# Two of four column blocks of an FFN down-projection by seven products in place of eight

## The chip, the cores and the metric

One Trainium2 chip, one of its cores. The metric is the device time of one execution in microseconds, as the median of several runs. TensorE (PE) multiplies matrices, VectorE (DVE), ScalarE (ACT) and GpSimd (POOL) work on elements, SyncE (SP) issues most DMAs. The profile adds PEld, TensorE's weight loads.

## The reference, cut to what matters

The program is a trunk of two layers on 256 positions and 2048 channels. Each layer has a mixer (pooling and attention in the first, an mLSTM in the second) and then the feed-forward network (FFN) that the change concerns; all of it is float32.

```
def conv_ffn(x, w_up, conv_w, conv_b, w_down):
    u = x @ w_up                                   # 2048 -> 2 x 5632
    up = jnp.pad(u, ((0, 0), (1, 1), (0, 0)))
    c = conv_w
    u = c[0] * up[:, :-2] + c[1] * up[:, 1:-1] + c[2] * up[:, 2:] + conv_b
    gate, val = jnp.split(u, 2, axis=-1)
    return (jax.nn.silu(gate) * val) @ w_down      # 5632 -> 2048
...
x = x + conv_ffn(rms_norm(x, norm_ffn[layer]), w_up[layer], conv_w[layer], conv_b[layer], w_down[layer])
```

## The kernel before

Every float32 operand of a product is split into a high part (a copy in TensorE's fp32r type) and a low part (the difference). A product is then three matmuls: high x high, high x low, low x high.

Weights come as a stream (class `Stream`, lines 65 to 108) of tiles of 128 partitions x 1024 columns, 512 KB each, in the order in which TensorE uses them. `load` issues a tile's DMA on SP into one of six buffers (tile `w`, line 80). `split` makes the high part on ScalarE (line 89) and the low part on VectorE (line 90) in one of four buffers (tile `hl`). So at most three split tiles stand ahead of the one that TensorE uses. `next` hands a tile to TensorE.

TensorE's order is that of the program, by hand; a small planner (`Weave`) puts the transposes and norm work of other tasks between the matmuls. The order on the other engines is written when the program is built, by a scheduler that places each instruction by a model of time; on the chip each engine then works through its list in order.

The FFN (`ffn_layer`, lines 877 to 962) has 44 feature blocks of 128, in chunks of 4, 8, 8, 8, 8, 8 (`FCH`). For each block, `up` (line 891) makes gate and value: `stat_group` (302) has four weight tiles, 64 matmuls of 512 or 256 columns, with the weights as the stationary operand; `gather` (363) joins the two partial sums from PSUM with a copy on ScalarE (366) and an addition on VectorE (367); line 895 multiplies by the norm R; line 899 applies the centre tap and the bias on ScalarE; lines 900 and 902 add the two outer taps on VectorE, once for the gate and once for the value; lines 905 to 908 make silu x value and split it into the chunk's tile `g`. `g` has two buffers, used by turns.

`down` (938) runs one chunk late: after the ups of chunk c come the four column blocks of 512 of chunk c-1 (the last chunk's follow at the end). For each column block and feature block, `mov_part` (325) has two row halves of 128 positions x three matmuls of 128x512 (tile `dn`), with activations stationary and weights moving; a weight tile holds two feature blocks, so it lasts 12 matmuls. `residual` (373) adds the sums into `x` on VectorE (376). PSUM has two pools of four banks: `mm`, two buffers of two banks, for up and down groups; `ps`, four buffers of one bank, for all smaller work. `_ffn_order` (1033) lists the weights in the same order.

Of the kernel before, what the change touches and what calls it, by code (L numbers as in the profile page):

```python
# [9 lines left out]
F32 = mybir.dt.float32  # L10
F32R = mybir.dt.float32r
AF = mybir.ActivationFunctionType
ALU = mybir.AluOpType
# [3 lines left out]
P = 128  # L17
D = 2048
S = 256
# [14 lines left out]
CH = 8  # L34
# [7 lines left out]
NB = D // 512  # L42
# [19 lines left out]
NC_ML = M_BG + 1  # L62


class Stream:


    def __init__(self, nc, wpool, spool, srcs, load_ahead, split_ahead):
        self.nc, self.wpool, self.spool, self.srcs = nc, wpool, spool, srcs
        self.la, self.sa = load_ahead, split_ahead  # L70
        self.w, self.hl = {}, {}
        self.n_load = self.n_split = self.at = 0

    def load(self, pieces=1):
        i = self.n_load
        width = self.srcs[i].shape[-1]
        n = width // pieces
        w = self.wpool.tile([P, CH * P], F32, tag="w", name=f"w{i}")
        for c in range(0, width, n):
            self.nc.sync.dma_start(w[:, c : c + n], self.srcs[i][:, c : c + n])  # L80
        self.w[i] = w, n, width
        self.n_load += 1

    def split(self, then=None):
        i = self.n_split
        w, n, width = self.w.pop(i)
        hl = self.spool.tile([P, 2, CH * P], F32R, tag="hl", name=f"hl{i}")
        for c in range(0, width, n):
            (self.nc.vector.tensor_copy if i + c == 0 else self.nc.scalar.copy)(hl[:, 0, c : c + n], w[:, c : c + n])  # L89
            self.nc.vector.tensor_sub(hl[:, 1, c : c + n], w[:, c : c + n], hl[:, 0, c : c + n].bitcast(F32))  # L90
            then and then(c // n)
        self.hl[i] = hl
        self.n_split += 1

    def ahead(self, i, split=None):
        n = len(self.srcs)
        while self.n_load < min(n, i + self.la + 1):
            if self.n_load >= self.n_split + self.la - self.sa + 1:
                self.split()
            self.load()  # L100
        while self.n_split < min(n, i + (self.sa if split is None else split) + 1):
            self.split()
# [54 lines left out]
def trunk(ctx: ExitStack, tc: tile.TileContext, gx, xT, xn, call, catt, cml, weights, out):  # L157
# [167 lines left out]
    def mov_part(ps, act, kts, first, last):  # L325

        n = len(kts)
        hl = None
        for i, k in enumerate(kts):
            if i % 2 == 0:  # L330
                hl = st.next()
            src, c = act(k), i % 2 * 512
            wh, wl = hl[:, 0, c : c + 512], hl[:, 1, c : c + 512]
            for t in range(2):
                xh, xl = (src[:, j, t * P : t * P + P] for j in range(2))
                mm(ps[:, t], xh, wh, first and i == 0, False)
                mm(ps[:, t], xh, wl, False, False)
                mm(ps[:, t], xl, wh, False, last and i == n - 1)
            wv.tick(1.29)
# [33 lines left out]
    def residual(ps, b, eng=None):  # L373
        for t in range(2):
            xs = x[:, t, b * 512 : b * 512 + 512]
            v.tensor_add(xs, xs, ps[:, t])
# [500 lines left out]
    def ffn_layer(layer, norm, nxt):  # L877
        with ExitStack() as es:
            def lp(name, bufs):
                return es.enter_context(tc.tile_pool(name=name, bufs=bufs, reuse_waits="tile"))  # L880

            tp = lp(f"ff{layer}", 2)

            def cw(tl, j):
                c = C_CONV + layer * 88 * 4 + tl * 4 + j
                return cst[:, c : c + 1]

            def xx(k):
                return norm.at(k)

            def up(f, gt, i):
                ps = stat_group(xx, list(range(KT)), f"up{layer}_{f}")
                wv.until(lambda: norm.R is not None)
                u = gather(tp, ps, f"up{layer}_{f}")
                v.tensor_mul(u, u, bc(norm.R, 2))  # L895
                y = tp.tile([P, 2, S], F32, tag="y", name=f"y{layer}_{f}")
                for j in range(2):
                    tl = f + j * FT
                    a.activation(y[:, j, :], u[:, j, :], AF.Identity, scale=cw(tl, 1), bias=cw(tl, 3))  # L899
                    v.scalar_tensor_tensor(y[:, j, 1:S], u[:, j, 0 : S - 1], cw(tl, 0), y[:, j, 1:S],  # L900
                                           ALU.mult, ALU.add)
                    v.scalar_tensor_tensor(y[:, j, 0 : S - 1], u[:, j, 1:S], cw(tl, 2), y[:, j, 0 : S - 1],  # L902
                                           ALU.mult, ALU.add)
                s_ = tp.tile([P, S], F32, tag="silu", name=f"s{layer}_{f}")
                a.activation(s_, y[:, 0, :], AF.Silu)
                v.tensor_mul(s_, s_, y[:, 1, :])
                a.copy(gt[:, i, 0, :], s_)
                v.tensor_sub(gt[:, i, 1, :], s_, gt[:, i, 0, :].bitcast(F32))

            def down_end(gt, b, kts):  # L910

                parts = [(0, 0, 512), (1, 0, 512)]
                pss = [psp.tile([P, 512], F32, tag="ps", name=f"end{i}") for i in range(2)]
                n = len(kts)

                def terms(i, k, hl):
                    t, c0, c1 = parts[i]
                    ps = pss[i][:, : c1 - c0]
                    wh, wl = (hl[:, j, k % 2 * 512 + c0 : k % 2 * 512 + c1] for j in range(2))
                    xh, xl = (gt[:, k, j, t * P : t * P + P] for j in range(2))  # L920
                    mm(ps, xh, wh, k == kts[0], False)
                    mm(ps, xh, wl, False, False)
                    mm(ps, xl, wh, False, k == kts[-1])

                for k in kts[:-2]:
                    if k % 2 == 0:
                        hl = st.next()
                    for i in range(2):
                        terms(i, k, hl)
                hl = st.next()  # L930
                for i, (t, c0, c1) in enumerate(parts):
                    for k in kts[-2:]:
                        terms(i, k, hl)
                    xs = x[:, t, b * 512 + c0 : b * 512 + c1]
                    v.tensor_add(xs, xs, pss[i][:, : c1 - c0])
                    nc.sync.dma_start(out[:, t, b * 512 + c0 : b * 512 + c1], xs)

            def down(c, gt, last):
                kts = list(range(FCH[c]))
                for b in range(NB):  # L940
                    if last and nxt is None and b == NB - 1:
                        down_end(gt, b, kts)
                        break
                    ps = mmp.tile([P, 2, 512], F32, tag="mm", name=f"dn{layer}_{c}_{b}")
                    mov_part(ps, lambda k: gt[:, k], kts, True, True)
                    residual(ps, b)
                    if last and nxt is None:
                        nc.sync.dma_start(out[:, :, b * 512 : b * 512 + 512], x[:, :, b * 512 : b * 512 + 512])
                    elif last:
                        nxt.add(b)  # L950

            wv.add(norm.finish(), 4.0)
            f, gts = 0, []
            for c, n in enumerate(FCH):
                gt = actp.tile([P, 8, 2, S], F32R, tag=f"B{c % 2}", name=f"g{layer}_{c}")
                gts.append(gt)
                for i in range(n):
                    up(f, gt, i)
                    f += 1
                if c:  # L960
                    down(c - 1, gts[c - 1], False)
            down(len(FCH) - 1, gts[-1], True)

    norms = [Norm(0), None]
    norms[1] = Norm(1)
# [16 lines left out]
def _mov(w):  # L982

    return w.reshape(-1, 2, P, 512).transpose(0, 2, 1, 3).reshape(-1, P, CH * P)
# [36 lines left out]
    return np.ascontiguousarray(t.transpose(4, 0, 2, 1, 3, 5)).reshape(FT * (KT // 4), P, CH * P)  # L1021


def _down_chunks(w):
    out, k0 = [], 0
    for n in FCH:
        rows = w[k0 * P : (k0 + n) * P]
        out += [_mov(rows[:, c : c + 512]) for c in range(0, D, 512)]
        k0 += n
    return np.concatenate(out)  # L1030


def _ffn_order():

    seq, u, d = [], 0, 0
    for c, n in enumerate(FCH):
        seq += [("u", u + i) for i in range(4 * n)]
        u += 4 * n
        if c:
            m = FCH[c - 1] // 4 * 8  # L1040
            seq += [("d", d + i) for i in range(m)]
            d += m
    m = FCH[-1] // 4 * 8
    seq += [("d", d + i) for i in range(m)]
    return seq


def _constants():
# [97 lines left out]
```

## Time and profile before

| | us |
|---|---|
| median of 3 runs (2206.41 to 2206.97) | 2206.9 |
| the profiled execution | 2206.69 |
| its span, first to last instruction | 2204.4 |
| TensorE busy in the span | 2199.3 |
| VectorE busy | 1525.3 |
| ScalarE busy | 1168.8 |
| matmuls of up groups (5632), busy | 984.2 |
| matmuls of down groups (2064), busy | 471.3 |
| low parts of weights on VectorE (772), busy | 939.0 |
| high parts of weights on ScalarE (771), busy | 806.1 |

The DMA queues moved 415.71 MB, 189 GB/s in the mean. A group line of the page reads: line of the kernel, engine, operation, tile written <- tiles read, partitions x elements, count | busy time in all, mean ns of one | idle time of the engine just before them, and who ended it. A line of the waits reads: who waited, for whom: us in all, times, the longest. A line of the view by windows gives the stretch, its length, and for each engine the busy time and the number of instructions, then the granted clock of TensorE, the busy share of the DMA engines and GB/s. The time that a matmul takes from issue to end (389 ns in the mean for a down matmul) is longer than the distance to the next one, since they are pipelined; the distance is what counts.

### The profile page before, as it was taken

The page shows a single profiled execution, that of the slowest core. Times are in us where ns is not written, and L with a number is a line of the kernel's source. Part 1 is how long each engine was busy: PE and PEld are TensorE (multiplying, and loading weights), DVE is VectorE, ACT ScalarE, POOL GpSimd, SP SyncE. Part 2 cuts the span into 40 slices and gives each one's busy share as a digit, 9 for nine tenths or more (in the row PEclk, how much of TensorE's full clock was granted, in tenths as well). Part 3 has the DMA queues.
Part 4 walks back from the last instruction along what each step waited for, and adds up shares of the span by engine and source line. Part 5 has one row for each costly group of instructions (what it writes and reads, how often), then busy time and mean ns, then how long its engine had stood idle before and what let it go on. Part 6 is the DMA issues. An engine that isn't in the chain of part 4 may idle for free.

```text
span 2204.4 us, 30654 instructions
## 1 busy us (share of the span) xinstructions
PE 2199.3 (100%) x11712; PEld 1888.3 (86%) x11712; DVE 1525.3 (69%) x2172; ACT 1168.8 (53%) x1666; POOL 28.1 (1%) x40
## 2 busy tenths in 40 slices
PE   9999999999999999999999999999999999999999
PEld 7888888888888888889888889888888888888887
DVE  7686677776776767666767677667777677676764
ACT  7665555554554545456555454555545455454542
POOL 0020000000000000000000000000000000000000
PEclk9999999999999999999999999999999999999999
DMA  9555566656566555656565655555666656566554
GB/s 324 177 165 168 176 191 188 191 188 197 184 194 187 191 192 191 197 171 207 162 197 178 186 180 168 185 180 188 188 191 190 196 186 192 190 191 191 192 191 143
DMA packets 118036, 415.71 MB, mean 189 GB/s; under 512 B 13082, under 2 KB 15426, under 8 KB 117890
## 3 DMA queue, kind: packets, MB, share of 16 engines
q1 hardware_dynamic: 114656, 409.76, 58.2%
q10 hardware_dynamic: 3074, 3.75, 0.8%
q8 instruction: 91, 1.49, 0.3%
q14 instruction: 55, 0.45, 0.1%
q0 software_dynamic: 160, 0.26, 0.0%
HBM read 411.58 MB, written 2.14 MB: 188 GB/s over the span
## 4 chain that ended last, share of the span: by engine, by line
PE 100%; DVE 0%; issue 0%
PE up L203 44%; PE dn L203 21%; PE op L203 8%; PE mv L203 4%; PE mq L203 4%; PE mk L203 4%; PE mo L203 4%; PE qproj L203 3%; PE kproj L203 1%; PE pool L203 1%; PE vproj L203 1%; PE qk L203 1%; PE av L203 1%; PE end L203 0%; PE xt L254 0%; PE sc L203 0%
## 5 line engine op out<-in xcount | busy, mean ns | idle before, releaser
L90 DVE TENSOR_TENSOR hl<-w,hl 128x1024 fp32r<-128x1024 f32 (+2 forms) x772 | 939.0, 1217 | 467.9 <-ACT hl L89 466.2
L89 ACT CAST hl<-w 128x1024 fp32r<-128x1024 f32 (+1 forms) x771 | 806.1, 1046 | 677.1 <-PE dn L203 242.6
L203 PE MATMUL up<-xx,hl 128*128 128x512 f32 (+1 forms) x5632 | 984.2, 337 | 0.0
L203 PEld LDWEIGHTS up<-xx,hl 128*128 128x128 f32 x5632 | 857.9, 188 | 125.8
L203 PE MATMUL dn<-hl,g 128*128 128x512 f32 x2064 | 471.3, 389 | 0.0
L203 PEld LDWEIGHTS dn<-hl,g 128*128 128x128 f32 x2064 | 386.3, 188 | 79.4
L366 ACT COPY tb_up<-up 128x512 f32<-128x512 f32 x88 | 51.7, 587 | 154.0 <-PE up L203 154.0
L367 DVE TENSOR_TENSOR tb_up<-up,tb_up 128x512 f32<-128x512 f32 x88 | 60.8, 691 | 97.1 <-ACT tb_up L366 97.1
L899 ACT ACTIVATE y<-tb_up,cst 128x256 f32<-128x256 f32 x176 | 96.4, 595 | 47.2 <-DVE tb_up L895 47.2
L203 PE MATMUL mk<-xx,hl 128*128 128x512 f32 (+1 forms) x512 | 92.2, 337 | 0.0
L203 PE MATMUL mq<-xx,hl 128*128 128x512 f32 (+1 forms) x512 | 92.1, 337 | 0.0
L203 PE MATMUL mv<-hl,xx 128*128 128x512 f32 (+2 forms) x480 | 91.7, 350 | 0.0
L203 PE MATMUL mo<-hl,xx 128*128 128x512 f32 (+1 forms) x480 | 91.6, 348 | 0.0
L203 PE MATMUL op<-hl,cat 128*128 128x512 f32 x384 | 91.6, 393 | 0.0
L203 PE MATMUL op<-hl,mcat 128*128 128x512 f32 x384 | 89.5, 392 | 0.0
L203 PEld LDWEIGHTS mq<-xx,hl 128*128 128x128 f32 x512 | 79.2, 188 | 11.6
L203 PEld LDWEIGHTS mk<-xx,hl 128*128 128x128 f32 x512 | 79.0, 188 | 11.4
L203 PEld LDWEIGHTS mv<-hl,xx 128*128 128x128 f32 x480 | 78.3, 189 | 11.2
L203 PEld LDWEIGHTS mo<-hl,xx 128*128 128x128 f32 x480 | 76.5, 190 | 10.6
L203 PEld LDWEIGHTS op<-hl,mcat 128*128 128x128 f32 x384 | 71.4, 188 | 14.6
L203 PEld LDWEIGHTS op<-hl,cat 128*128 128x128 f32 x384 | 70.9, 188 | 14.1
L902 DVE SCALAR_TENSOR_TENSOR y<-tb_up,cst,y 128x255 f32<-128x255 f32 x176 | 76.8, 477 | 0.0
(209 smaller groups left out, 1270.0 us busy)
## 6 DMA issues: line engine op xcount, KB each, us to landing
w<-in_up SPq DMA_DIRECT2D x352, 512.0 KB, 3.5
w<-in_dn SPq DMA_DIRECT2D x176, 512.0 KB, 3.7
w<-in_m_in SPq DMA_DIRECT2D x124, 512.0 KB, 4.0
w<-in_a_in SPq DMA_DIRECT2D x46, 512.0 KB, 4.5
w<-in_a_out SPq DMA_DIRECT2D x32, 512.0 KB, 3.5
w<-in_m_out SPq DMA_DIRECT2D x32, 512.0 KB, 3.4
w<-in_m_g SPq DMA_DIRECT2D x5, 432.0 KB, 3.4
x<-in_xn SPq DMA_DIRECT2D x4, 512.0 KB, 9.9
```

Of the source, the lines that this page charges most:

```text
L89: (self.nc.vector.tensor_copy if i + c == 0 else self.nc.scalar.copy)(hl[:, 0, c : c + n], w[:, c : c + n])
L90: self.nc.vector.tensor_sub(hl[:, 1, c : c + n], w[:, c : c + n], hl[:, 0, c : c + n].bitcast(F32))
L203: pe.matmul(out_, lhsT, rhs, start=start, stop=stop, skip_group_check=True)
L366: a.copy(tb, ps[:, :, 1, :])
L367: v.tensor_add(tb, ps[:, :, 0, :], tb)
L899: a.activation(y[:, j, :], u[:, j, :], AF.Identity, scale=cw(tl, 1), bias=cw(tl, 3))
L902: v.scalar_tensor_tensor(y[:, j, 0 : S - 1], u[:, j, 1:S], cw(tl, 2), y[:, j, 0 : S - 1], ALU.mult, ALU.add)
```

## The change

For all chunks but the last of each layer, the column blocks 2 and 3 (columns 1024 to 2047) are no longer done by `down`. A pair of feature blocks (k), the two row halves (t) and the two column blocks form a 2x2 by 2x2 product of blocks, which is done by a scheme of seven products with sums of blocks in place of eight products.

The combinations of activations (`combine`) are made on VectorE after every second up, and split by ScalarE and VectorE. The combinations of weights are made as the tiles come in: a tile `Sum` is one load on SP and a second load on POOL that adds to it in the DMA; a tile `Chain`, which follows it, gets two additions on VectorE before it is split. The seven products go into seven banks that gather over a whole chunk, in two passes: pass A (four products, one `Sum` and one `Chain` tile for each pair) and pass B (three products, one and a half plain tiles). A unit of pass A stands after each of the next chunk's first four ups, a unit of pass B after each of the other four. At a pass's end the banks are added into a tile `acc` (on VectorE; copied by ScalarE for the first chunk), and after the last chunk but one `total` adds the seven sums into `x`. The column blocks 0 and 1 keep the old scheme, and stand after the second and the fourth up of the next chunk (the first chunk has two pairs; its units and down groups follow half as many ups). The last chunk is done as before.

In `up`, the outer taps are now products on ScalarE (tile `z`, two more activations for the gate and two for the value) and two additions on VectorE that cover gate and value at once.

```
@@ class Stream
     def load(self, pieces=1):
+        src = self.srcs[i]
+        if isinstance(src, Sum):
+            i in self.w or self.prepare(i)
+            return
+        src = src.src if isinstance(src, Chain) else src
...
+    def prepare(self, i):
+        w = self.sums.tile([P, CH * P], F32, tag="sum", name=f"sum{i}")
+        self.nc.sync.dma_start(w, self.srcs[i].one)
+        self.nc.gpsimd.dma_start(w, self.srcs[i].other, accum_op=ALU.add)
+        self.w[i] = w, CH * P, CH * P
 
     def split(self, then=None):
         i = self.n_split
         w, n, width = self.w.pop(i)
+        if isinstance(self.srcs[i], Sum):
+            self.sum = w
+        elif isinstance(self.srcs[i], Chain):
+            half = CH * P // 2
+            self.nc.vector.tensor_add(w[:, :half], w[:, :half], self.sum[:, :half])
+            self.nc.vector.tensor_add(w[:, half:], w[:, half:], w[:, :half])
...
     def ahead(self, i, split=None):
         n = len(self.srcs)
+        for j in range(self.n_load, min(n, i + 10)):
+            if isinstance(self.srcs[j], Sum) and j not in self.w:
+                self.prepare(j)
@@ def ffn_layer
-            tp = lp(f"ff{layer}", 2)
+            tp, t1p, kp = lp(f"ff{layer}", 2), lp(f"ff1{layer}", 1), lp(f"ffk{layer}", 1)
+            st.sums = lp(f"ffs{layer}", 2)
...
+                z = t1p.tile([P, 2, 2, S], F32, tag="z", name=f"z{layer}_{f}")
                 for j in range(2):
                     tl = f + j * FT
+                    a.activation(z[:, 0, j, :], u[:, j, :], AF.Copy, scale=cw(tl, 0))
+                    a.activation(z[:, 1, j, :], u[:, j, :], AF.Copy, scale=cw(tl, 2))
                     a.activation(y[:, j, :], u[:, j, :], AF.Identity, scale=cw(tl, 1), bias=cw(tl, 3))
-                    v.scalar_tensor_tensor(y[:, j, 1:S], u[:, j, 0 : S - 1], cw(tl, 0), y[:, j, 1:S],
-                                           ALU.mult, ALU.add)
-                    v.scalar_tensor_tensor(y[:, j, 0 : S - 1], u[:, j, 1:S], cw(tl, 2), y[:, j, 0 : S - 1],
-                                           ALU.mult, ALU.add)
+                v.tensor_add(y[:, :, 1:S], y[:, :, 1:S], z[:, 0, :, 0 : S - 1])
+                v.tensor_add(y[:, :, 0 : S - 1], y[:, :, 0 : S - 1], z[:, 1, :, 1:S])
...
+            def combine(c, j, g4):
+                sf = t1p.tile([P, 4, P], F32, tag="sf", name=f"sf{layer}_{c}_{j}")
+                v.tensor_sub(sf[:, 0:2], g4[:, 0::3], g4[:, 1:2].to_broadcast([P, 2, P]))
+                v.tensor_add(sf[:, 2], sf[:, 1], g4[:, 0])
+                v.tensor_sub(sf[:, 3], sf[:, 2], g4[:, 2])
+                s3 = kp.tile([P, 2, 3, P], F32R, tag=f"s3{j}", name=f"s3{layer}_{c}_{j}")
+                s1 = st.sums.tile([P, 2, P], F32R, tag=f"s1{j}", name=f"s1{layer}_{c}_{j}")
+                for d, e in ((s3, sf[:, 0:3]), (s1, sf[:, 3])):
+                    a.copy(d[:, 0], e)
+                    v.tensor_sub(d[:, 1], e, d[:, 0].bitcast(F32))
...
+            def product(ps, xs, wh, wl, first, last):
+                xh, xl = xs
+                mm(ps, xh, wh, first, False)
+                mm(ps, xh, wl, False, False)
+                mm(ps, xl, wh, False, last)
+                wv.tick(0.68)
+
+            def unit(kind, c, j):
+                order = (4, 6, 5, 3) if kind == "A" else (0, 1, 2)
+                if j == 0:
+                    for e in order:
+                        pss[e] = psp.tile([P, 512], F32, tag="ps", name=f"pp{layer}_{c}_{e}")
...
+                for m, e in enumerate(order):
+                    if m % 2 == 0:
+                        hl = st.next()
+                    wh, wl = (hl[:, i, m % 2 * 512 : m % 2 * 512 + 512] for i in range(2))
+                    product(pss[e], xs[m], wh, wl, j == 0, j == n - 1)
+                if j == n - 1:
+                    for e in order:
+                        if c == 0:
+                            a.copy(acc[:, e], pss[e])
+                        else:
+                            v.tensor_add(acc[:, e], acc[:, e], pss[e])
+                    if kind == "B" and c == len(FCH) - 2:
+                        total()
+
+            def total():
+                p1, p2, p3, q4, p5, q6, p7 = (acc[:, e] for e in range(7))
+                x00, x01, x10, x11 = (x[:, t, c : c + 512] for t in range(2) for c in (1024, 1536))
+                v.tensor_sub(q6, q6, p1)
+                v.tensor_sub(p5, q6, p5)
+                for xs, op, e in ((x01, v.tensor_add, p5), (x01, v.tensor_sub, p3), (x11, v.tensor_add, p5),
+                                  (x11, v.tensor_sub, p7), (x10, v.tensor_sub, q6), (x10, v.tensor_add, p7),
+                                  (x10, v.tensor_add, q4), (x00, v.tensor_add, p1), (x00, v.tensor_add, p2)):
+                    op(xs, xs, e)
...
+def _ffn_plan():
+    seq = []
+    for c, n in enumerate(FCH):
+        pairs = FCH[c - 1] // 2 if c else 0
+        for i in range(n):
+            seq.append(("up", c, i))
+            if i < 2 * pairs:
+                seq.append(("AB"[i // pairs], c - 1, i % pairs))
+            for b in range(2):
+                if pairs and i == (b + 1) * pairs // 2 - 1:
+                    seq.append(("down", c - 1, b))
+    return seq + [("down", len(FCH) - 1, b) for b in range(NB)]
...
@@ weights of a pair, b11 to b22 its blocks of 128 x 512
+    return np.concatenate(out), two(b12, b12), two(b11, b22), two(b22, b21), two(b11, b21), b22
...
+        elif kind == "A":
+            out += [Sum(s0[q], s1[q]), Chain(r[q])]
+        else:
+            out += [ba[q], bb[q]]
```

## The prediction

> **What bounds the kernel now.** I read the page's chain first, then the waits of TensorE, then one stretch of the stage that the change touches, then the rows of the instructions concerned.
>
> ```profile
> PE 2199.3 (100%) x11712; PEld 1888.3 (86%) x11712; DVE 1525.3 (69%) x2172; ACT 1168.8 (53%) x1666; POOL 28.1 (1%) x40
> ...
> PE 100%; DVE 0%; issue 0%
> ```
>
> The chain of work that ended last is TensorE from end to end. The waits of TensorE alone confirm it: one wait, 1.2 us, in the whole execution.
>
> ```profile
> PE wps L227 <- DVE pad L595: 1.2, 1, 1.2
> ```
>
> So a matmul taken away shortens the run by its whole duration, as long as nothing else becomes late. The next view says how near the others are. Its middle row is one steady FFN chunk (eight up groups, four down groups); the other two are stretches in which VectorE is nearly or quite full.
>
> ```profile
> core 0: us, PE busy (x) PEld busy (x) DVE busy (x) ACT busy (x) POOL busy (x), PEclk, DMA share, GB/s
> 140.00:168.00 28.00, 28.00 (x176) 24.98 (x175) 25.54 (x50) 20.14 (x44) 9.00 (x11) 1.00 0.48 143
> 433.00:566.00 133.00, 133.00 (x708) 114.16 (x707) 91.20 (x120) 68.28 (x89) 0.00 (x0) 1.00 0.60 191
> 1092.00:1106.00 14.00, 14.00 (x65) 11.60 (x64) 14.00 (x13) 6.29 (x7) 0.00 (x0) 1.00 0.50 171
> ```
>
> The reader is to see that a chunk has VectorE 69% and ScalarE 51% busy at a granted clock of 1.00, and that TensorE stays full beside a VectorE at 91% (25.54 of 28 us, ScalarE 72%) and, for 14 us, at 100%. Four split tiles in flight carry it over such stretches. The prices come from the rows by shape, the page's down row, the chain's stretch of eight ups, the same chunk for the down tiles (`dn`) alone, and the DMA rows:
>
> ```profile
> L90 DVE TENSOR_TENSOR hl<-w,hl 128x1024 fp32r<-128x1024 f32 x762 | 930.6, 1222 | 464.5 <-ACT hl L89 462.8
> L902 DVE SCALAR_TENSOR_TENSOR y<-tb_up,cst,y 128x255 f32<-128x255 f32 x176 | 76.8, 477 | 0.0
> L895 DVE TENSOR_TENSOR tb_up<-tb_up,R 128x512 f32<-128x512 f32 x88 | 60.9, 692 | 3.0
> L908 DVE TENSOR_TENSOR g<-s,g 128x256 fp32r<-128x256 f32 x88 | 36.7, 417 | 0.0
> ```
> ```profile
> L203 PE MATMUL dn<-hl,g 128*128 128x512 f32 x2064 | 471.3, 389 | 0.0
> ```
> ```profile
> 413.14 89.16 PE up L203 x512
> ```
> ```profile
> 433.00:566.00 133.00, 43.69 (x192) 35.97 (x192) 5.14 (x8) 1.00 0.60 191
> ```
> ```profile
> L899 ACT ACTIVATE y<-tb_up,cst 128x256 f32<-128x256 f32 x176 | 96.4, 595 | 47.2 <-DVE tb_up L895 47.2
> ```
> ```profile
> w<-in_dn SPq DMA_DIRECT2D x176, 512.0 KB, 3.7
> ...
> R<-rr POOLq DMA_DIRECT2D x2, 128.0 KB, 6.5
> ```
>
> **The change, part by part.**
>
> *Removed on the path.* Per pair of feature blocks, two column blocks and two row halves cost 8 products of 3 matmuls; now 7. All chunks but the last hold 36 feature blocks, 18 pairs a layer, 36 in both: 36 x 3 = 108 matmuls of 128x512. The down row of the page gives 471.3 us / 2064 = 0.228 us each; in the chunk above the same tiles take 43.69 us for 192, also 0.228. 108 x 0.228 = **24.6 us**. The other products keep their shape and price.
>
> *VectorE.* From the rows, 1.07 ns per element on top of a fixed part: 0.28 us for 128 elements, 0.417 for 256, 0.555 for 384, 0.69 for 512, 1.222 for 1024. An up group: four low parts 4.89, gather and R 1.38, the two joined tap additions 2 x 0.69 (four of 0.477 before), gate and low part 0.83: 8.5 us. Each A unit adds two low parts and two chain additions, 2 x 1.222 + 2 x 0.69 = 3.8; each B unit 1.222 + 0.686 = 1.9; the combinations of a pair 0.417 + 3 x 0.28 + 0.555 = 1.8, half to each up; sums out of PSUM 7 x 0.685 = 4.8 a chunk; a down group 4 x 1.222 + 2 x 0.683 = 6.25. A chunk: 4 x (8.5 + 3.8 + 0.9) + 4 x (8.5 + 1.9 + 0.9) + 2 x 6.25 + 4.8 = 115.3 us. By the same means the old chunk is 97.2, where the view shows 91.20: successive instructions overlap a little, so times 0.938, **108 us**. TensorE's new chunk: 8 x 11.15 (89.16 us per eight ups in the chain) + 84 x 0.228 + 2 x 10.9 = 130.2 us. VectorE rises from 69% to 83%; an up with its A unit is the tightest, 13.2 x 0.938 = 12.4 of 13.9 us (89%), and the two down groups in the A pass give back 4.7 us each. That lies below the 91% over 28 us at which TensorE did not wait. The final sum (11 additions of 0.69, 7.6 us) falls beside the last chunk's four down groups, where VectorE has 4.7 us to spare in each.
>
> *ScalarE.* Four more activations per up (two per half, taken at 0.595, the row with two column operands; 0.47 would be the low end by the plain scaled rows), 1.5 more casts per pair, the two casts of the combinations at 0.8: a chunk goes from 71 to 100 us nominal, times 0.96 as before: 96 of 130 us, 74%. Hidden beside TensorE too. Behind the six activations of an up stand the casts of the next tiles, 6 x 0.595 = 3.6 us late at most; a tile's slot comes free three tiles ahead of its use, 8 us in ups, 5 where the short tiles of a unit lie between. If that cover were gone the price is 3.6 us per up at most.
>
> *SP and POOL.* 36 first loads of sums (512 KB) and 36 half tiles go on SP, 36 accumulating loads on POOL. In the order of instructions the first sums of each layer stand among the preceding output projection's loads, and wait there for the last head's operations; in the trace those end at 189.5 us, and the load behind it on SP left at 189.8, so nothing is held. Later sums wait for the buffer of the sum two before, which was split before the loads beside it in the queue may go. POOL's square roots stand behind the first two sums, over 60 us before they are due. Bytes: 36 x 1.25 MiB = 47 MB more; a chunk moves 25.3 + 5.2 = 30.5 MB in 130 us, 235 GB/s, and by the view's 0.60 at 190 a DMA share of 0.74 (0.77 in the A pass). The page's first slice moved 324 GB/s, so plain loads keep up.
>
> *The accumulating load* is in no row. From below: a plain load of the same bytes, 3.7 us. From above: POOL's 128 KB row taken in proportion, 4 x 6.5 = 26 us. I take 8, nearer to the first since 6.5 us for a quarter of the bytes must be mostly fixed. Its cover: of each chunk's four sums, two have a buffer early; the other two get theirs when the sum two before is split, and VectorE's chain addition stands behind the first split of the second-next up: about an up (less one tile), a unit, a down and one tile, 8.4 + 2.7 + 10.9 + 2.8 = 25 us, less 4 for the first load: 21 us, and 4 to 5 more until TensorE runs out of split tiles.
>
> *Sum.* 2206.7 us (the profiled execution; its span 2204.4, the median of the runs 2206.9) - 24.6 + 2.4 (one wait of the 1.2 us kind in each layer, where units begin) = **2184.5 us**.
>
> **The rivals.**
>
> *VectorE sets the pace of the stage.* In the old chunk it idled 41 us, nearly all of it for ScalarE:
>
> ```profile
> DVE hl L90 <- ACT hl L89: 30.8, 28, 1.6
> DVE tb_up L367 <- ACT tb_up L366: 8.8, 8, 1.1
> ```
>
> The new one has 130.2 - 108.2 = 22 us left. For: the joined tap additions wait for all six activations, and both engines run in a fixed order. Against: it idled because it was ahead, waiting for slots, and such waits shrink when it is late; the two full stretches above. If 24 us of waits stay, each of the nine chunk-equivalents (4.5 a layer) grows by 2 us, 18 in all: 2202 us; from 24.7 us on the gain is gone, and at 26 it is 2220.
>
> *The sums land late: slower.* Where the accumulating load takes more than 25.5 us from issue to landing, VectorE's in-order queue stands at the chain addition with the splits of the next tiles behind it, and TensorE follows. That is 2 sums in 4 chunks of 2 layers, 16 places; the gain is gone at 27 us, and at 28 it is 16 x 2.5 = 40 us: 2184.5 + 40 = about 2224. For: POOL's DMA rows are the slowest per byte, 6.5 us for 128 KB, and VectorE will be busier. Against: the 8 us estimate.
> The Trainium skill ("SBUF — State Buffer", section "Who interferes with whom") speaks for this rival: GpSimd writes such a DMA's descriptors, and VectorE operations that hold the shared port shut it out. Its strict form needs two-port operations, and these rows are all TENSOR_TENSOR; with two SBUF inputs it names a conflict with GpSimd reads only. The POOL rows agree in direction (6.5 against 3.7 us); no run here shows the cause.
>
> *It does not do what it says:* the short tiles of a unit could cost TensorE between products what eight products would. Nothing in the old rows shows it (op and dn, with the same three-matmul terms, both run at 0.23 us); 2200 to 2207.
>
> **How the numbers follow.** Forecast 0.57 (2182 to 2190); VectorE's pace 0.20 (half of it faster than 2202, a quarter on each side of 2211); late sums 0.20, nearly all slower; no effect 0.03. A measurement here tells 0.2% (4.4 us) from no change. Faster: 0.57 + 0.10 = 0.67; same: 0.05 + 0.01 + 0.03 = 0.09; slower: 0.05 + 0.19 = 0.24. The range runs from 2181 (no waits at all) to 2222; it leaves out half of the late sums, the worst of VectorE's pace, and little below.
>
> **What would show it.** Right: TensorE's waits still a few us, the products' tiles at 0.228 us per matmul, a VectorE of 80 to 85% in a chunk, chunks of 130 us. VectorE's pace: TensorE waiting for low parts (hl) all through the stage, chunks over 132 us. Late sums: VectorE idle at the chain additions, released by the accumulating DMA, landings over 25 us in the DMA rows. I am wrong if the chain of waits leaves TensorE for more than 10 us.

## The result, and the profile after

The changed kernel takes 2203.78 us (median of 20 runs, 2202.42 to 2206.86), the kernel before, beside it, 2206.58 us (20 runs, 2206.35 to 2206.97): a ratio of 0.9987, 95% interval 0.9981 to 0.9993. So 2.8 us are gained where 22.2 were forecast, and by the prediction's bound of 0.2% (4.4 us) that is no difference. The time lies in the range that was given, 2181 to 2222, but the forecast was wrong by 19.3 us.

The page of the changed kernel, in the same order as before: busy times, the clock by slices, and the shares of the chain of waits.

```profile
PE 2181.5 (99%) x11604; PEld 1871.5 (85%) x11604; DVE 1669.3 (76%) x2358; ACT 1374.3 (62%) x2176; POOL 59.2 (3%) x76
...
PEclk9999999999999999999999999999999999999998
...
PE 98%; DVE 1%; issue 0%; ACT 0%; DVEq 0%
```

108 matmuls are gone (x11712 to x11604), as the change says. The span fell from 2204.4 to 2201.9 us, but TensorE's busy time fell by 17.8. (It did not fall by the 24.6 of the 108 matmuls: what is left runs some 1.9 us slower, and some 24 matmuls ran at half the clock; both are shown below.) The clock's last slice is 8 where it was 9, and the chain, all TensorE before, now leaves it for some 2% of the span. TensorE's waits say where:

```profile
PE dn L237 <- ACT g L948: 15.2, 2, 7.6
PE wps L261 <- DVE pad L629: 1.2, 1, 1.2
```

Two waits of 7.6 us, one in each layer, for ScalarE's cast of the activations `g`; the 1.2 us one was there before. So there is one place to look at. The steady chunks are as forecast. The view by windows of one chunk (ups of eight blocks, units A and B, two down groups), and under it its two passes:

```profile
core 0: us, PE busy (x) PEld busy (x) DVE busy (x) ACT busy (x) POOL busy (x), PEclk, DMA share, GB/s
541.50:671.70 130.20, 130.20 (x694) 111.61 (x693) 106.96 (x144) 87.55 (x137) 3.44 (x4) 1.00 0.75 234
541.50:618.90 77.40, 77.40 (x401) 65.94 (x400) 66.36 (x88) 52.50 (x81) 3.44 (x4) 1.00 0.81 245
618.90:671.70 52.80, 52.80 (x294) 45.67 (x293) 40.60 (x57) 35.05 (x56) 0.00 (x0) 1.00 0.66 219
```

TensorE is full at a granted clock of 1.00, from the first `up` of the chunk to the first of the next in 130.2 us (forecast 130.2); VectorE is busy 107 us (forecast 108) and 86% in pass A. The load that no row had shown, and the load it adds to, in the DMA rows (last figure: median us from issue to landing):

```profile
sum<-in_dn SPq DMA_DIRECT2D x36, 512.0 KB, 4.7
sum<-in_dn POOLq DMA_DIRECT2D x36, 512.0 KB, 7.6
```

It lands after 7.6 us (taken at 8).

**The gap.** TensorE's timeline at the end of the first layer's ups (start, duration, operation, in brackets the wait ahead of it; `pp` are the products of a unit); the last up's matmuls end at 930.1 us:

```profile
929.95 1.53 PE L237 MATMUL pp<-hl,g 128*128 128x512 f32 x6
931.32 0.85 PE L237 MATMUL pp<-hl,s 128*128 128x512 f32 x3
932.00 9.68 PE L237 MATMUL dn<-hl,g 128*128 128x512 f32 x42
949.31 6.87 PE L237 MATMUL dn<-hl,g 128*128 128x512 f32 x18 [7.62 <-ACT g L948]
```

Behind the last up stand one unit B (9 matmuls) and then the last chunk's first down group. Its first seven feature blocks (42 matmuls) run; the eighth needs the last up's own activations. ScalarE has written their high part at 949.25 us, 19.1 us after the up's end, and VectorE the low part at 949.91, after 19.8. VectorE in these 19 us:

```profile
930.76 0.69 DVE L401 TENSOR_TENSOR tb_up<-up,tb_up 128x512 f32<-128x512 f32 x1 [1.10 <-ACT tb_up L400]
931.37 1.27 DVE L1000 TENSOR_TENSOR acc<-acc,pp 128x512 f32<-128x512 f32 x2
...
934.90 0.68 DVE L1008 TENSOR_TENSOR acc<-acc 128x512 f32<-128x512 f32 x1
935.50 0.68 DVE L1013 TENSOR_TENSOR x<-x,acc 128x512 f32<-128x512 f32 x1
936.11 2.35 DVE L121 TENSOR_TENSOR hl<-w,hl 128x1024 fp32r<-128x1024 f32 x2
...
939.58 0.68 DVE L941 TENSOR_TENSOR y<-y,z 128x510 f32<-128x510 f32 x1
...
943.05 1.89 DVE L1013 TENSOR_TENSOR x<-x,acc 128x512 f32<-128x512 f32 x3
944.86 0.68 DVE L942 TENSOR_TENSOR y<-y,z 128x510 f32<-128x510 f32 x1
945.46 1.22 DVE L121 TENSOR_TENSOR hl<-w,hl 128x1024 fp32r<-128x1024 f32 x1
946.60 1.89 DVE L1013 TENSOR_TENSOR x<-x,acc 128x512 f32<-128x512 f32 x3
948.40 0.41 DVE L947 TENSOR_TENSOR s<-s,y 128x256 f32<-128x256 f32 x1
```

The reader is to see two kinds of work in one list. The last up's own (L401, L933, L941, L942, L947, then L949) is short; between its pieces stand the eleven additions of the final sum (L1008, L1009, L1013), the three of the pass's banks (L1000) and six splits (L121). VectorE hardly pauses (it is busy 7.60 of 7.60 and 7.70 of 7.70 us in the windows further down). In the kernel before, the same place was (TensorE, then VectorE):

```profile
900.22 56.16 PE L203 MATMUL dn<-hl,g 128*128 128x512 f32 x247
```
```profile
908.10 0.42 DVE L908 TENSOR_TENSOR g<-s,g 128x256 fp32r<-128x256 f32 x1
```

The low part, last of the activations, was there 8.1 us after the up's end (900.4 us), and TensorE had four down groups of the chunk before (4 x 10.9 us) and seven blocks of the last chunk's first, some 53 us, to do meanwhile. The change took the path to the low part from 8.1 to 19.8 us, and its cover from 53 to 11.6.

**The clock behind it.** The view by windows around the gap:

```profile
934.00:941.60 7.60, 7.60 (x34) 6.01 (x33) 7.60 (x11) 5.24 (x8) 0.00 (x0) 1.00 0.56 180
941.60:949.30 7.70, 0.09 (x1) 0.00 (x0) 7.70 (x13) 0.82 (x2) 0.00 (x0) 0.68 0.66 226
949.40:954.50 5.10, 5.10 (x12) 3.99 (x13) 2.74 (x5) 2.20 (x4) 0.00 (x0) 0.50 0.19 60
954.70:957.00 2.30, 2.30 (x12) 1.88 (x11) 0.00 (x0) 0.79 (x1) 0.00 (x0) 1.00 0.53 116
```

The granted clock (the column before the DMA share) falls to 0.50 in the gap and stays there for 5.3 us behind it: 12 matmuls in 5.1 us, 0.427 each from start to start in place of 0.227, some 2.4 us more. In the trace the half clock lasts 10.24 us each time and begins 2.7 us into the gap. The Trainium skill ("TensorE: Matmul & The Clock Gate", Part 1) says that TensorE falls to half speed after an idle window of some 3.4 us and comes back after a busy one. The length agrees, with three times 3.41 us, and so does the return; the fall came earlier than an idle window of that length, 2.7 us into the gap, and in experiment 1 a wait of 1.8 us was enough.

A gap of 7.62 us between the end of one matmul and the start of the next puts their starts 8.0 us apart in place of 0.23, so it costs 7.8. Each gap costs 7.8 + 2.4 us, 20.4 in all, and 2203.8 - 20.4 = 2183.4 us would be the kernel without them. That is the theory: the final sum and the missing down groups together make the gap. The rivals: one of the two alone makes it, or the gap hides another cost that would come out once it is closed.

### The profile page after: what moved, and what is told of

It is laid out like the page before. It is cut to its first block, busy times and chain, and to the rows that moved or that the text cites. A ratio compares the mean times of both kernels' runs of the same rounds, so it can differ in the third digit from the quotient of the medians.

```text
span 2201.9 us, 31410 instructions
## 1 busy us (share of the span) xinstructions
PE 2181.5 (99%) x11604; PEld 1871.5 (85%) x11604; DVE 1669.3 (76%) x2358; ACT 1374.3 (62%) x2176; POOL 59.2 (3%) x76
## 4 chain that ended last, share of the span: by engine, by line
PE 98%; DVE 1%; issue 0%; ACT 0%; DVEq 0%
PE up L237 45%; PE dn L237 12%; PE op L237 8%; PE pp L237 8%; PE mv L237 4%; PE mq L237 4%; PE mk L237 4%; PE mo L237 4%; PE qproj L237 3%; PE pool L237 1%; PE kproj L237 1%; PE vproj L237 1%; DVE hl L121 1%; PE qk L237 1%; PE av L237 1%; PE end L237 0%
## 5 line engine op out<-in xcount | busy, mean ns | idle before, releaser
L121 DVE TENSOR_TENSOR hl<-w,hl 128x1024 fp32r<-128x1024 f32 (+2 forms) x808 | 951.8, 1193 | 263.9 <-ACT hl L120 261.6
L120 ACT CAST hl<-w 128x1024 fp32r<-128x1024 f32 (+2 forms) x807 | 817.3, 1028 | 458.7 <-PE up L237 138.7
L237 PEld LDWEIGHTS up<-xx,hl 128*128 128x128 f32 x5632 | 867.0, 188 | 130.4
L237 PE MATMUL dn<-hl,g 128*128 128x512 f32 x1200 | 282.7, 395 | 15.2 <-ACT g L948 15.2
L237 PEld LDWEIGHTS dn<-hl,g 128*128 128x128 f32 x1200 | 228.1, 191 | 64.1 <-ACT g L948 16.1
L237 PE MATMUL pp<-hl,s 128*128 128x512 f32 x432 | 111.2, 393 | 0.0
L401 DVE TENSOR_TENSOR tb_up<-up,tb_up 128x512 f32<-128x512 f32 x88 | 60.7, 690 | 55.2 <-ACT tb_up L400 55.2
L941 DVE TENSOR_TENSOR y<-y,z 128x510 f32<-128x510 f32 x88 | 60.6, 689 | 52.4 <-ACT y L940 51.8
L938 ACT ACTIVATE z<-tb_up,cst 128x256 f32<-128x256 f32 x176 | 88.6, 503 | 12.6 <-DVE tb_up L933 12.3
L237 PEld LDWEIGHTS pp<-hl,s 128*128 128x128 f32 x432 | 78.5, 188 | 15.1
L237 PEld LDWEIGHTS mq<-xx,hl 128*128 128x128 f32 x512 | 79.2, 188 | 11.6
L237 PEld LDWEIGHTS mk<-xx,hl 128*128 128x128 f32 x512 | 79.0, 188 | 11.4
```

The costliest lines, as they stand in the source:

```text
L237: pe.matmul(out_, lhsT, rhs, start=start, stop=stop, skip_group_check=True)
L401: v.tensor_add(tb, ps[:, :, 0, :], tb)
L938: a.activation(z[:, 0, j, :], u[:, j, :], AF.Copy, scale=cw(tl, 0))
L941: v.tensor_add(y[:, :, 1:S], y[:, :, 1:S], z[:, 0, :, 0 : S - 1])
```

## The experiments

All were timed in five rounds beside the kernel before (2206.57 us beside numbers 1, 2, 5 and 6, 2206.67 beside 3, 4, 7 and 8). Edits are against the changed kernel where nothing else is said.

**1. The final sum left out.**

```
-                    if kind == "B" and c == len(FCH) - 2:
-                        total()
```

> Edit: the eleven additions that add the seven sums into x are left out, so that the two column blocks lack what the seven products of the first five chunks give. The order of TensorE stays. Theory A (VectorE has these additions, 6.6 us of them, ahead of the last up's tap additions and gate, and they alone make its activations late): the wait shrinks to about 1 us, the clock stays, 2184 to 2187 us. Rival C (the way of the last up through gather, six activations, two additions, silu and split is itself too long for the 11.7 us that one unit and seven eighths of a down group give): a wait of 4 us or more stays in each layer and the clock still drops, 2193 us or more.

Measured: 2187.63 us (2186.39 to 2188.10), ratio 0.9913 (0.9899 to 0.9927). TensorE's waits:

```profile
PE dn L237 <- ACT g L948: 1.8, 1, 1.8
PE wps L261 <- DVE pad L629: 1.2, 1, 1.2
PE dn L237 <- DVE g L949: 0.6, 1, 0.6
```

Without the eleven additions the activations' low part comes 13.8 and 12.9 us after the up's end in the two layers, and 15.2 us of waiting become 2.4. The rival (the last up's own way is too long by 4 us or more, 2193 us or more) falls by its numbers, and no further cost comes out behind the gap. But at 13 us the path is still longer than its cover of 11.6, and the 1.8 us wait is followed by 3.41 us at half clock: leaving out the sum alone does not quite close the gaps.

**2. One down group put between.** `_ffn_plan` holds back the second old-scheme down group of the fifth chunk.

```
-                if pairs and i == (b + 1) * pairs // 2 - 1:
+                if pairs and i == (b + 1) * pairs // 2 - 1 and (c < len(FCH) - 1 or b == 0):
                     seq.append(("down", c - 1, b))
+    seq.append(("down", len(FCH) - 2, 1))
```

> Edit: the second old-scheme down group of the last chunk but one is held back and stands between the last unit of pass B and the last chunk's first down group; nothing else changes. Theory (the 22 us that are missing against the forecast are two gaps of TensorE, one in each layer, where the last chunk's first down group waits 7.6 us for the activations of the last up, and each gap also halves the granted clock for 10.2 us, of which some 5 us beside matmuls cost 2.4 us more): with 10.9 us of other matmuls in between the activations are ready in time, both gaps go, and the time is 2203.8 - 2 x (7.8 + 2.4) = 2183.4 us; clock 1.00. Rival (the units make the whole FFN stage slower, by VectorE's pace): 2200 to 2204.

Measured: 2188.53 us (2188.2 to 2193.4), ratio 0.9925 (0.9912 to 0.9939), not the 2183.4 expected. TensorE's waits, and VectorE's line for the last low part of `g`:

```profile
PE dn L237 <- DVE g L949: 3.6, 2, 2.2
PE wps L261 <- DVE pad L629: 1.2, 1, 1.2
PE dn L237 <- ACT g L948: 0.4, 2, 0.2
```
```profile
944.30 0.40 DVE L949 TENSOR_TENSOR g<-s,g 128x256 fp32r<-128x256 f32 x1
```

The cover grew by 10.9 us, but the last up now ends at 919.2 us and the low part comes 25.5 us later (24.8 in the second layer), not 19.8: with one more group in the program, the order written at build time puts four more splits and that group's two additions ahead of it (six splits in the changed kernel, ten here). The gap was not simply shortened by what was put into it: waits of 2.2 and 1.4 us are left, at a clock of 1.00.

**3. Both down groups put between.**

```
-                if pairs and i == (b + 1) * pairs // 2 - 1:
+                if pairs and i == (b + 1) * pairs // 2 - 1 and c < len(FCH) - 1:
                     seq.append(("down", c - 1, b))
+    seq += [("down", len(FCH) - 2, b) for b in range(2)]
```

> The changed kernel with both old-scheme down groups of the fifth chunk held back: they stand between the last unit and the first down group of the last chunk, so that some 33 us of TensorE's work (2 of the unit, 21.8 of the two groups, 9.5 of the last chunk's own first seven blocks) lie between the last up and the first matmul that needs its activations. Theory (the cover was too short: the activations come 19.3 us after the up's end in the changed kernel, and at about 25 us where one group was held back, since the order of VectorE then puts more splits ahead of them): both waits and the clock drops go, 2203.8 - 2 x (7.8 + 2.4) = 2183.4 us, 2182.5 to 2185, and TensorE's only wait is the 1.2 us one. Rival (the order slides along with every group that is put in between, so that a wait of 2 us a layer stays): 2187 to 2189, as with one group held back. Second rival (the A units of that chunk, with no down group between them, make VectorE late): waits for low parts of weight tiles, over 2186.

Measured: **2183.62 us** (2183.18 to 2184.09), ratio 0.9895 (0.9881 to 0.9908). The page's busy line, its chain, and the waits of TensorE:

```profile
PE 2176.4 (100%) x11604; PEld 1868.7 (86%) x11604; DVE 1668.0 (76%) x2358; ACT 1374.7 (63%) x2176; POOL 59.3 (3%) x76
...
PE 100%; DVE 0%; issue 0%
```
```profile
PE wps L261 <- DVE pad L629: 1.2, 1, 1.2
```

The same 11604 matmuls and VectorE within 2 us of the changed kernel's busy time, yet 20.2 us less. The low part still comes 25.5 us after the up's end (933.78 to 934.18 against 908.65), so the order did not slide any further (ten splits again), and 33 us cover it. The A units of that chunk, now without a down group between them, did not make VectorE late. This is the best version of the study.

**4. One group between, and the last unit an up earlier**, so that the final sum begins before the last up.

```
+    last = ("B", len(FCH) - 2, FCH[-2] // 2 - 1)
+    seq.remove(last)
+    seq.insert(seq.index(("up", len(FCH) - 1, FCH[-1] - 1)), last)
     seq.append(("down", len(FCH) - 2, 1))
```

> One down group held back as in the first experiment, and the last B unit one up earlier, so that the final sum's eleven additions begin an up (8.3 us of TensorE) before the last up ends. Theory (what holds the last activations is that the final sum and the splits stand ahead of them on VectorE): the 2.2 us waits that one group held back left grow smaller, 2183.5 to 2186 us. Rival (VectorE's order puts the activations behind the splits whatever the sum does): as the first experiment, 2187 to 2189.

Measured: 2185.11 us (2184.5 to 2185.59), ratio 0.9902 (0.9888 to 0.9915).

```profile
PE wps L261 <- DVE pad L629: 1.2, 1, 1.2
PE dn L237 <- DVE g L949: 0.6, 1, 0.6
PE up L237 <- DVE hl L121: 0.4, 1, 0.4
```

The sum out of the way, the low part comes 21.7 and 19.0 us after the up's end in place of 25.5 and 24.8, and 3.4 us of the 4.9 that separate experiment 2 from 3 are gone. So the sum's place on VectorE matters with the group in between as well. ("The first experiment" of the expectation is number 2 here.)

**5. The gap filled.** 33 useless matmuls (33 x 0.228 = 7.5 us) ahead of the eighth block: TensorE is busy while it would wait.

```
+            if fill and i == n - 1:
+                fp = psp.tile([P, 512], F32, tag="ps", name="fill")
+                for _ in range(fill):
+                    mm(fp, act(kts[0])[:, 0, :P], hl[:, 0, :512], True, True)
...
-                mov_part(ps, lambda k: gt[:, k], kts, True, True)
+                mov_part(ps, lambda k: gt[:, k], kts, True, True, 33 if last and b == 0 else 0)
```

> Edit: the changed kernel with 33 matmuls of no use (7.5 us at full clock, into a bank of their own) ahead of the last feature block of the last chunk's first down group, so that TensorE works through the gap. It adds work and waits as long as before for the same activations. Theory (part of each gap's cost is the halved clock behind it): the clock stays at 1.00 and 2 x 2.4 = 4.8 us are gained, 2199 us. If the clock's fall costs nothing: 2203.8 or a little more.

Measured: 2199.44 us (2199.23 to 2200.32), ratio 0.9968 (0.9956 to 0.9981); 66 matmuls more, and 4.3 us less than the changed kernel. The view by windows over the same place and behind it:

```profile
940.00:949.00 9.00, 9.00 (x42) 7.43 (x40) 9.00 (x13) 1.47 (x2) 0.00 (x0) 1.00 0.67 217
949.00:956.00 7.00, 6.85 (x32) 5.16 (x31) 4.33 (x9) 3.94 (x8) 0.00 (x0) 1.00 0.40 112
```

The clock stays at 1.00. That closes the account by spans: 2201.9 - 2197.5 = 4.4 us is the half clock, 2197.5 - 2181.6 (experiment 3) = 15.9 us the two gaps (15.2 of it are the waits), 20.3 in all.

**6. The final sum on GpSimd.**

```
-                v.tensor_sub(q6, q6, p1)
+                g.tensor_sub(q6, q6, p1)
...
```

(and so for all eleven.)

> Edit: the same eleven additions on GpSimd in place of VectorE. Theory A: as without them, 2184 to 2187 us, if GpSimd's additions, which I put at 1 to 2 us each, end before the third down group adds to the same columns (22 us after the first begins), and do not hold VectorE up. If they share VectorE's way to the memory and slow it, the wait comes back in part: up to 2195. Rival C: 2193 or more.

Measured: 2210.59 us (2209.46 to 2211.58), ratio 1.0017 (1.0009 to 1.0026), 6.8 us slower than the changed kernel and far above the highest time expected (2195 for the shared way to the memory), though VectorE has eleven operations less ahead of the activations. The timelines of GpSimd and of VectorE at the place:

```profile
933.41 1.29 POOL L1008 TENSOR_TENSOR acc<-acc 128x512 f32<-128x512 f32 x1 [103.29 <-DVE acc L1000]
...
938.60 15.89 POOL L1013 TENSOR_TENSOR x<-x,acc 128x512 f32<-128x512 f32 x8
```
```profile
941.88 1.77 DVE L941 TENSOR_TENSOR y<-y,z 128x510 f32<-128x510 f32 x1
943.58 2.30 DVE L121 TENSOR_TENSOR hl<-w,hl 128x1024 fp32r<-128x1024 f32 x1
945.80 1.74 DVE L942 TENSOR_TENSOR y<-y,z 128x510 f32<-128x510 f32 x1
947.47 2.29 DVE L121 TENSOR_TENSOR hl<-w,hl 128x1024 fp32r<-128x1024 f32 x1
949.68 1.48 DVE L947 TENSOR_TENSOR s<-s,y 128x256 f32<-128x256 f32 x1
```

Beside GpSimd's additions a VectorE operation with two inputs in SBUF takes about 1.07 us more: a split 2.30 in place of 1.22, a tap addition 1.75 in place of 0.68, the gate 1.48 in place of 0.41 (two in each layer grew by less, L933 by 0.73 and one split by 0.50). GpSimd's own additions grow from 1.29 to some 2 us. The last gate ends 19.8 us after the up's end, later than with the sum on VectorE (18.7). TensorE's wait for the high part is 7.2 us (7.6 before), but it then waits 2.0 us more for the low part and 1.2 us for a split tile in each layer; with 0.7 us for another split, its waits grow by 6.2 us in all. The Trainium skill ("SBUF — State Buffer", section "Who interferes with whom") says that a VectorE instruction with two SBUF inputs contends with a GpSimd instruction that reads SBUF; the trace agrees, and gives the price.

**7. The taps alone**, in the kernel before: the four activations and two joined additions per up, with no product less (the part of the diff in `up`, nothing else).

> The kernel before with the outer taps on ScalarE alone: four activations more and two joined additions in place of four on VectorE for each up, no product less. My reading: both engines are beside TensorE, nothing on the path changes: 2206.6 us, within 1 us. Rival (the six activations delay the casts of weight tiles): TensorE waits for hl, 2208 or more.

Measured: 2206.77 us (2206.36 to 2206.96), ratio 1.0000 (0.9991 to 1.0009). Moving the taps costs no time and brings none by itself. VectorE's line for the last low part of the first layer's `g`:

```profile
910.67 0.42 DVE L909 TENSOR_TENSOR g<-s,g 128x256 fp32r<-128x256 f32 x1
```

It comes 10.9 us after the up's end (900.24) in place of 8.1. So with the taps on ScalarE the last up's path is 2.7 us longer; here the four down groups cover that. Of the 11.7 us by which the path grew in the changed kernel, these 2.7 go with the taps, 6.0 to 6.7 with the final sum (experiment 1), and the other 2 to 3 were not tried one by one; the additions of the banks are among them. Each kernel has its own order on VectorE, so this is a rough account.

**8. The scheme with the old taps**, and one group between as in experiment 2.

```
-                    a.activation(z[:, 0, j, :], u[:, j, :], AF.Copy, scale=cw(tl, 0))
-                    a.activation(z[:, 1, j, :], u[:, j, :], AF.Copy, scale=cw(tl, 2))
...
+                    v.scalar_tensor_tensor(y[:, j, 1:S], u[:, j, 0 : S - 1], cw(tl, 0), y[:, j, 1:S],
+                                           ALU.mult, ALU.add)
...
```

> The scheme of seven products with one down group held back, but the outer taps on VectorE as before. It tells whether the taps had to move for the scheme to pay: VectorE has per up 4 x 0.477 in place of 2 x 0.69 (0.5 us more) and 108 + 4 = 112 of 130 us busy in a chunk. If VectorE has slack in the chunks and the activations' path after the last up is about as long, 2188.5 us as with the taps moved, within 1.5. If the slack is thin: waits for hl in the chunks, 2192 or more.

Measured: 2187.98 us (2186.81 to 2189.59), ratio 0.9915 (0.9902 to 0.9929), the same as experiment 2 (2188.53). The chunk by windows, to be held against the first line of the changed kernel's:

```profile
541.50:671.70 130.20, 130.20 (x694) 111.64 (x693) 108.77 (x159) 76.17 (x105) 3.44 (x4) 1.00 0.75 234
```

VectorE has 1.8 us more, ScalarE 11.4 less, TensorE is full: the taps did not have to move for the scheme to pay. The equal times hide two differences. The last low part comes 24.0 us after the up's end, in place of 25.5 and 24.8, and TensorE's waits for `g` are 2.3 us in place of 4.0; but elsewhere it waits for low parts of weights, as it does not in experiment 2:

```profile
PE up L237 <- DVE hl L121: 1.9, 3, 1.1
```

This is the sign that was named for thin slack, though the time stays well below the 2192 us named with it.

## Why the prediction was wrong, point by point

- *The step that failed* reads: "The final sum (11 additions of 0.69, 7.6 us) falls beside the last chunk's four down groups, where VectorE has 4.7 us to spare in each." The price was right (0.68 us for one, 6 to 7 us of path for the eleven). The place was wrong: the first of those four groups needs the last up's own activations in its eighth block, and the sum stands ahead of them on VectorE. The step counted room on an engine over a stretch, where it had to ask what TensorE needs first within it. And it did not ask what the moved down groups had covered: the old order had four of them, 43.7 us, between the last up and the last chunk's first down group. Experiments 1, 2, 3 and 5 show this: the sum makes the path 6 to 7 us longer, the missing groups make the length count, and with both groups of the fifth chunk between the last up and its use the time is 2183.62 us. That this is only 0.9 below the forecast is partly luck: two errors in the sum, of 2.4 and 1.9 us (next point), nearly cancel.
- *Removed on the path*: right. From before to experiment 3 the span falls by 22.8 us, of 24.6 for 108 matmuls. The rest: from the start of a product's matmul to the next matmul's it is 0.2298 us, for a `dn` matmul 0.2273 (means of 756 and 1200 in that trace); 756 x 0.0025 = 1.9 us. The 2.4 us of waits that were put at the units' beginning are not there.
- *VectorE* in a chunk: 107 us measured, 108 forecast; TensorE's chunk 130.2, 130.2. *ScalarE*: 87.6 against 96; an outer tap's activation takes 0.50, near the low end that was named (0.47), where the centre tap with its two column operands takes 0.59. "Hidden beside TensorE too" holds in the steady chunks; after the last up the moved taps are part of the path that nothing hid (2.7 us, experiment 7).
- *VectorE's pace* (2202 us) did not come: TensorE waits for no low part of a weight in the whole execution. (By its own terms, 22.2 us over nine chunks, the gain would be gone at 24.5 us of waits, not 24.7.) *Late sums* (2224) did not come either: the load lands after 7.6 us in the median and 10.6 at most, not 25, and no wait of TensorE goes back to it. VectorE does wait 42.8 us in all at the chain additions, for the plain load of the second tile; that is hidden. Not all VectorE rows shown are TENSOR_TENSOR, as that rival says: L902 is not, and the change takes it out.
- *It does not do what it says* (2200 to 2207) holds the measured time, for a reason that isn't so: the products of the short tiles run at 0.230 us per matmul. A time that fits a rival does not show its mechanism.
- The condition given for being wrong, a chain that leaves TensorE for more than 10 us, is what came.

## What to carry to other kernels

When work that stands between a producer and its consumer is taken away or moved, count what it covered: here the four groups between the last up and its use were worth more than any engine's busy share showed. At the end of a stage, list for TensorE's next matmuls which operands are still being made, and what stands ahead of them on VectorE; a steady stretch with 18% of VectorE free says nothing of that. If a gap is to be filled, put in more than its length, because the order on the other engines moves with the program (10.9 us put into a gap of 7.6 left 2.2 and 1.4).

## What the runs showed of the hardware

- A gap of 7.6 us on TensorE cost 2.2 us more behind it, through a granted clock of 0.50 for 10.24 us from 2.7 us into the gap. Short waits can do it too: in experiment 1 a wait of 1.8 us was followed by 3.41 us at half clock, while the two of 2.2 and 1.4 us in experiment 2 were not; what tells them apart was not tried. In the traces the clock changes only after whole multiples of 3.413 us (275, 3, 352, 3 and 10 of them in the changed kernel).
- Elementwise work on GpSimd beside VectorE is not free: most VectorE operations with two SBUF inputs grew by 1.07 us whatever their size (256 to 1024 elements), the two in each layer that read PSUM did not (0.68 us for 512 elements, as without it). GpSimd's additions all had 512 elements, so whether the 1.07 us depends on their length was not tried.
- A load that adds to what lies in SBUF landed after 7.6 us for 512 KB, beside 4.7 for the plain one.
